# A two-layer token mixer: one more empty step in two side lanes, and small matmuls gathered into fewer steps

## The chip, the cores and the metric

The kernel runs on one core of a Trainium2 chip. The metric is the device time of one launch in microseconds (us). The engines are named as in the profile: PE is TensorE (matmul), PEld its weight loads, DVE is VectorE, ACT is ScalarE, POOL is GpSimd, SP is SyncE, which here issues the weight DMAs.

## The reference, cut to what matters

Two layers over 256 positions and 2048 channels. The even layer mixes with HGRN2 (a gated linear recurrence, 8 heads of 128 keys) and RG-LRU (a gated scan after a causal convolution, 8 blocks of 128) side by side; the odd layer is mLSTM (8 heads, 128 keys, 256 values). Each layer ends with an output projection, a residual add and a gated embedding of a second input `p`.

```python
h = x
for i in range(2):
    hn = rmsnorm(h, norm[i])
    if i == 0:
        q, f, v, z, xb, zb = split(hn @ e_w_in)          # 2048 -> 6 x 1024
        ya = head_rmsnorm(hgrn2(q, f, v, lb)) * silu(z)
        xc = causal_conv(xb, w, b)                        # 4 taps
        r, g = sigmoid(xc @ w_r + b_r), sigmoid(xc @ w_i + b_i)   # per block of 128
        a = exp(-8 * r * softplus(-lam))
        yb = scan(a, sqrt(1 - a * a) * (g * xc)) * silu(zb)
        mix = concat(ya, yb) @ e_w_out
    else:
        q, k, v, og, z, ig, fg = split(hn @ o_w_in)
        q, k = silu(causal_conv(q, k))
        yc = mlstm(q, k, v, ig, log_sigmoid(fg))          # (q k' * weights) v / max(|den|, exp(-m))
        mix = (head_rmsnorm(yc) * sigmoid(og) * silu(z)) @ o_w_out
    h = h + mix
    h = h + sigmoid(h @ ple_gate_w[i]) * rmsnorm(p[i] @ ple_w[i])
return rmsnorm(h)
```

All in fp32.

## The kernel before, in words

**The main line.** Nearly all time goes into projections of 256 tokens by weights that come from memory once. A float32 product is made of three: the weight piece (`raw`, 128x1024, 512 KB, by SP's queue) is rounded by ACT (`whi`, L123), the remainder is taken by DVE (`wlo`, L124), and the activations are kept as `ahl`, a rounded part and a remainder side by side. `whi` and `wlo` have four buffers each, two blocks' worth. `block` (L147) makes 128 output channels for all tokens: 16 matmuls with `whi` (L155, 128x512), then `pump()`, then 16 with `wlo` (L162, 128x256). `merge` (L179, L180) adds the two halves of its bank, `project` (L190) multiplies by the norm's factor. `project_tok` (L193) has tokens on the partitions and two banks: for each of four quarters of the inputs (`kq` 0 to 3) 12 matmuls into the first bank (L208 to L210), `pump()`, and 12 into the second. `gate_tok` calls it for a gate and follows it with a tanh (ACT, L444) and a product (DVE, L445) for each bank.

**The side lanes.** The rest of the work is written as Python generators that stand in named lanes: "att" (HGRN2's attention of four heads, called a pair g here, `attention(g)`), "rg" (`rg_lru(r, xc)`), "mix" (`mix(j)`, mLSTM of two heads), "tr" (`turn`), "fm", "norm" and others. Every `pump()` advances each lane to its next `yield`, and the matmuls of that step stand in PE's program between the `whi` and the `wlo` matmuls of one block. So a `yield` is the unit of delay: it puts what follows it one block later. When a generator of a lane ends, the next one's first step runs in the same pump. The tile scheduler then orders each engine by what is ready, and the casts L123 and L124 have a priority.

**The lanes that the change touches**, by the lines of the kernel before:
- `attention` (L524): `qf = q * f` on DVE (L530, 128x1024), a yield, then five levels B = 1, 2, 4, 8, 16. Each level's matmuls (L546; at B = 1 L541 too) read `qf` and `k`, then DVE multiplies half of `qf` (L553) and half of `k` (L554) by the level's factors and forms the next factors (L556), a yield. After the levels come one more step of matmuls (L605, L610), and `read_out` (from L628) with the values, whose normalisation on DVE is a dozen small operations (L216 to L222, L644, L648) and a product (L650).
- `rg_lru` (L662): waits a step, and then for j = 0, 1 makes two gate products from `xc`, the convolution's output, each of two matmuls in a bank of its own (L674), followed by sigmoids on ACT (L678), and a yield. Then tanh, exp, square (L684 to L690), a square root (L693), and the scan (DVE, L696). `xc` is made by `conv`: one ACT operation (L705) and three of DVE (L708) for each 128 channels.
- `mix` (L864): decay weights, two empty steps, then the scores of two heads (L887, L888; DVE multiplies them by the weights, L889), a yield, then the read-out with the values (L899, L901), from which ACT copies and squares and DVE copies one column (L904), a yield.
- `turn` (L1018): turns two 128x512 halves of the residual by four transposes each (L1023), a yield after each half.

**PSUM.** Three pools: "mm" with three banks for projections, "mx" with three and "st" with two for the side lanes. A side step that takes a bank waits until its last reader is done.

Of the kernel before, what the change touches and what calls it, by code (L numbers as in the profile page):

```python
# [11 lines left out]
F32 = mybir.dt.float32  # L12
# [4 lines left out]
ALU = mybir.AluOpType  # L17
PSUM = bass.MemoryType.PSUM

P = 128  # L20
# [24 lines left out]
def trunk(ctx: ExitStack, tc: tile.TileContext, a, out):  # L45
    nc = tc.nc
    v, s, gp, te, sy = nc.vector, nc.scalar, nc.gpsimd, nc.tensor, nc.sync
# [7 lines left out]
    px = ctx.enter_context(tc.tile_pool(name="px", bufs=3, space=PSUM))  # L55
    pst = ctx.enter_context(tc.tile_pool(name="pst", bufs=2, space=PSUM))
# [7 lines left out]
    def start(lane, gen):  # L64
        lanes.setdefault(lane, []).append(gen)
# [374 lines left out]
    def gate_tok(w, j, act, u):  # L440
# [6 lines left out]
    mx, e0, e1, lb, omb, sp, ez, z2, pol, sp8, spm8 = (small(8, n) for n in (  # L447
        "mx", "e0", "e1", "lb", "omb", "sp", "ez", "z2", "pol", "sp8", "spm8"))
# [37 lines left out]
    with m0_scope:  # L486
# [37 lines left out]
        def attention(g):  # L524
# [2 lines left out]
            Ac = m0.tile([P, 4, P], F32, name="Ac", tag="Ac", bufs=1)  # L527
            C = m0.tile([P, 8, 32], F32, name="C", tag="C", bufs=1)
            qf = m0.tile([P, 1024], F32, name="qf", tag="qf", bufs=1)
            v.tensor_tensor(out=qf, in0=q, in1=f, op=ALU.mult)  # L530
            if g == 0:
                gp.memset(A, 0.0)
# [2 lines left out]
            for B in LEVELS:  # L535
                ps = px.tile([P, 512], F32, name="mx", tag="mx")
                if B == 1:
                    for c in range(8):
                        for x in range(0, P, 32):
                            o = c * P + x  # L540
                            te.matmul(ps[x:x + 32, 128 + c * 32:160 + c * 32], k[:, o:o + 32], q[:, o:o + 32],  # L541
                                      start=True, stop=True)
                for c in range(8):
                    for x in range(0, P, 32):
# [3 lines left out]
                                  start=True, stop=True)  # L548
# [28 lines left out]
            for i in (1, 0):  # L577
                v.tensor_tensor(out=sx[:, :, i], in0=sx[:, :, i + 1], in1=t4[:, :, 0, i + 1], op=ALU.mult)
                j = 3 - i
# [17 lines left out]
            for b in range(2):  # L597
                ps = px.tile([P, 512], F32, name="mx", tag="mx")
# [8 lines left out]
            ps = pst.tile([P, 512], F32, name="st", tag="st")  # L607
# [54 lines left out]
        def rg_lru(r, xc):  # L662
            bw = m0.tile([P, 2, 512], F32, name="bw", tag="bw", bufs=1)
            sy.dma_start(out=bw, in_=a["bw"][r])
            av = m0.tile([P, 1024], F32, name="av", tag="f")
            tt = m0.tile([P, 1024], F32, name="tt", tag="k")
            it = m0.tile([P, 1024], F32, name="it", tag="it", bufs=1)
            yield
            for j in range(2):
                for w, (dst, bias) in enumerate(((av, "bbr"), (it, "bbi"))):  # L670
                    ps = px.tile([P, 512], F32, name="mx", tag="mx")
                    for i in range(2):
                        c = 2 * j + i
                        te.matmul(ps[:, i * T:(i + 1) * T], bw[:, w, c * P:(c + 1) * P], xc[:, c * T:(c + 1) * T],  # L674
                                  start=True, stop=True)
                    for i in range(2):
                        c = 2 * j + i
                        s.activation(dst[:, c * T:(c + 1) * T], ps[:, i * T:(i + 1) * T], AF.Sigmoid,  # L678
                                     bias=pc(bias, 4 * r + c))
                yield  # L680
            for c in range(4):
                b = 4 * r + c
                cc = slice(c * T, (c + 1) * T)
                s.activation(tt[:, cc], av[:, cc], AF.Tanh, scale=sp8[:, b:b + 1])  # L684
                s.activation(av[:, cc], av[:, cc], AF.Exp, scale=spm8[:, b:b + 1])
            v.tensor_tensor(out=it, in0=it, in1=xc, op=ALU.mult)
            for j in range(2):
                sq = tp.tile([P, 512], F32, name="sq", tag="sq")
                jj = slice(j * 512, (j + 1) * 512)
                s.activation(sq, av[:, jj], AF.Square)  # L690
                v.scalar_tensor_tensor(tt[:, jj], sq, 1.0, tt[:, jj], op0=ALU.add, op1=ALU.mult)
            yield
            s.activation(tt, tt, AF.Sqrt, scale=0.25)  # L693
            v.tensor_tensor(out=it, in0=it, in1=tt, op=ALU.mult)
            v.memset(av.rearrange("p (c t) -> p c t", t=T)[:, :, 0:1], 0.0)
            v.tensor_tensor_scan(tt, av, it, 0.0, op0=ALU.mult, op1=ALU.add)  # L696
            res["h", r] = tt
# [13 lines left out]
        vts = [i_proj(0), i_proj(1)]  # L711
# [47 lines left out]
    with tc.tile_pool(name="m1", bufs=2) as m1:  # L759
# [20 lines left out]
        vts = []  # L780
        for j in range(4):
            psv = project_tok(a["ov"], j, acth)

            vt = m1.tile([P, 2, 2, VW], F32, name="vt", tag="vt", bufs=6)
# [9 lines left out]
        ps = pm.tile([P, 512], F32, name="mm", tag="mm")  # L794
        for hf in range(2):
            wt = wp.tile([P, 1024], F32R, name="whi", tag="whi")
# [8 lines left out]
            for kk in range(8):  # L805
                k = hf * 8 + kk
                for i, x in enumerate(acth[k // 2][0:2]):
                    te.matmul(ps[:, 0:T], wt[:, kk * P:(kk + 1) * P], x[:, k % 2],
                              start=(k == i == 0), stop=(k == KT - 1 and i == 1))
# [42 lines left out]
        SC = 0.25 * 128.0 ** -0.5  # L852
# [11 lines left out]
        def mix(j):  # L864

            if j == 0:
                spread(0)
                spread(1)
                yield
            p3 = spr[j]  # L870
            wt = m1.tile([P, 2, 384], F32, name="wt", tag="wt", bufs=1)
            v.tensor_tensor(out=wt[:, :, 0:T], in0=tri2.unsqueeze(1).to_broadcast([P, 2, T]), in1=p3, op=ALU.subtract)
            v.tensor_tensor(out=wt[:, :, T:384], in0=tri2[:, 0:P].unsqueeze(1).to_broadcast([P, 2, P]),
                            in1=p3[:, :, P:T], op=ALU.subtract)
            for i in range(2):
                hd = 2 * j + i
                s.activation(wt[:, i, 0:T], wt[:, i, 0:T], AF.Exp, bias=aT[:, hd:hd + 1])
                s.activation(wt[:, i, T:384], wt[:, i, T:384], AF.Exp, bias=aT[:, 8 + hd:9 + hd])
            if j < 2:
                spread(j + 2)  # L880
            yield
            yield
            scw = m1.tile([P, 2, 384], F32, name="scw", tag="scw", bufs=2)
            for i in range(2):
                q, k = qk[j][:, i * T:(i + 1) * T], qk[4 + j][:, i * T:(i + 1) * T]
                sc = px.tile([P, 512], F32, name="mx", tag="mx")
                te.matmul(sc[:, 0:T], k[:, 0:P], q, start=True, stop=True)  # L887
                te.matmul(sc[:, T:384], k[:, P:T], q[:, P:T], start=True, stop=True)  # L888
                v.scalar_tensor_tensor(scw[:, i, :], sc[:, 0:384], SC, wt[:, i, :], op0=ALU.mult, op1=ALU.mult)  # L889
            yield  # L890

            vt = vts[j]
            nm = m1.tile([P, 2, 512], F32, name="num", tag="vt", bufs=6)
            for i in range(2):
                pool, tag = ((px, "mx"), (pst, "st"))[i]
                for hf in range(2):
                    c = hf * 8 + 2 * j + i
                    ps = pool.tile([P, 512], F32, name="nu", tag=tag)[:, 0:VW]
                    te.matmul(ps, scw[:, i, hf * P:(hf + 1) * P], vt[:, 0, i], start=True, stop=(hf == 0))  # L899
                    if hf:  # L900
                        te.matmul(ps, scw[:, i, T:384], vt[:, 1, i], start=False, stop=True)  # L901
                    o = nm[:, hf, i * 256:(i + 1) * 256]
                    s.copy(o, ps[:, 0:256])
                    v.tensor_copy(den[:, c:c + 1], ps[:, 256:VW])  # L904
                    sq = tp.tile([P, 512], F32, name="sq", tag="sq")[:, 0:256]
                    s.activation(sq, ps[:, 0:256], AF.Square, accum_out=ss[:, c:c + 1])
            nums[j] = nm
            yield

        def mix_norm():  # L910


            t, r, yh = (m1.tile([P, 16], F32, name=n, bufs=1) for n in ("nwt", "nwr", "nwy"))
            s.activation(den, den, AF.Abs)
            v.tensor_tensor(out=den, in0=den, in1=aT[:, 16:32], op=ALU.max)
            v.tensor_scalar(den, den, 1e21, EPS ** 0.5, op0=ALU.min, op1=ALU.mult)
            v.tensor_tensor(out=den, in0=den, in1=den, op=ALU.mult)
            v.scalar_tensor_tensor(den, ss, 1.0 / 256, den, op0=ALU.mult, op1=ALU.add)
            newton(den, t, r, yh)
            for hf in range(2):  # L920
                c = slice(hf * 8, hf * 8 + 8)
                v.tensor_scalar(fac[:, c], r[:, c], norm["rt"][:, hf:hf + 1], 0.25, op0=ALU.mult, op1=ALU.mult)
            yield

        y = {}
        for j in range(4):
            qk[j] = qk_proj(j)
            qk[4 + j] = qk_proj(4 + j)
            start("mix", mix(j))
        start("mix", mix_norm())  # L930
        held = []
        for j in range(4):
# [85 lines left out]
        def turn(q, banks):  # L1018

            for hf in range(2):  # L1020
                ps = px.tile([P, 512], F32, name="mx", tag="mx")
                for i in range(4):
                    te.transpose(ps[:, i * P:(i + 1) * P], hq[q][:, i * T + hf * P:i * T + (hf + 1) * P], ident)  # L1023
                banks.append(ps)
                yield

        def gated(n, ps, tr, pl, hf, on_act=True):
            th = tp.tile([P, 512], F32, name="th", tag="th")[:, 0:pl.shape[1]]
# [182 lines left out]
```

## Time and profile before

| what | us |
| --- | --- |
| median of 3 runs | 1079.74 (1079.16 to 1080.49) |
| the profiled execution | 1078.11 |
| its span | 1076.3 |
| PE busy | 1055.6 |
| DVE busy | 735.1 |
| ACT busy | 584.8 |
| POOL busy | 67.8 |

The profiled execution is one launch; its span goes from the first to the last instruction. A row of a timeline gives the start, the length, the engine and line, the operation with its tiles and shape, the count of equal instructions, and in brackets idle time just before with what ended it. PE writes two records for a matmul of plain float32 operands, so `x8` at L674 is four matmuls. PE's rows overlap (the next matmul starts before the last one's modelled end), so its costs are read from start to start.

### The profile page before, as it was taken

What the parts mean: (1) busy time and instruction counts of PE and PEld (TensorE: products, weight loads), DVE (VectorE), ACT (ScalarE), POOL (GpSimd) and SP (SyncE); (2) the same over time, 40 slices, a digit from 0 to 9 for tenths busy, and PEclk for the clock granted to TensorE, in tenths of its full rate; (3) what the DMA queues carried; (4) which work ended last, traced back from release to release, by engine and by line L of the source; (5) the groups of instructions that cost most, each with busy time, mean ns of one, the idle gap of its engine ahead of it and who ended that gap; (6) DMA issues with size and microseconds to landing.
All of it is one profiled execution on the core that took longest, in us unless ns stands there. A gap on an engine that the chain in (4) does not pass through costs nothing.

```text
span 1076.3 us, 16798 instructions
## 1 busy us (share of the span) xinstructions
PE 1055.6 (98%) x6500; PEld 910.4 (85%) x6500; DVE 735.1 (68%) x1106; ACT 584.8 (54%) x863; POOL 67.8 (6%) x72
## 2 busy tenths in 40 slices
PE   7999999999999999999999999999999999999996
PEld 6888888887888888888888888888888888888886
DVE  6868978877767557777544887855456677555665
ACT  7565455688654435556444666654445554434543
POOL 0140400000000000112000000000000000000111
PEclk9999999999999999999999999999999999999998
DMA  9667444445655555555654655545555755555552
GB/s 337 166 230 217 153 160 149 154 138 194 240 195 193 193 186 188 185 189 194 195 193 158 216 188 167 176 157 195 195 195 190 247 184 181 196 192 176 181 176 79
DMA packets 56576, 201.76 MB, mean 187 GB/s; under 512 B 6472, under 2 KB 6864, under 8 KB 56496
## 3 DMA queue, kind: packets, MB, share of 16 engines
q1 hardware_dynamic: 54720, 195.04, 54.1%
q0 software_dynamic: 1776, 5.65, 1.8%
q8 instruction: 51, 0.84, 0.3%
q14 instruction: 29, 0.24, 0.1%
HBM read 198.55 MB, written 2.11 MB: 186 GB/s over the span
## 4 chain that ended last, share of the span: by engine, by line
PE 93%; DVE 2%; ACT 2%; issue 1%; DMA 1%; SPq 0%; DVEq 0%; ACTq 0%
PE mm L155 31%; PE mm L162 16%; PE mm L208 12%; PE mm L209 12%; PE mm L210 12%; DVE wlo L124 1%; PE mm L1065 1%; PE mm L1064 1%; PE mm L1063 1%; PE nu L899 1%; PE mx L546 1%; DMA raw<-in_pw_dram 1%; PE mx L428 0%; ACT whi L123 0%; PE mm L143 0%
## 5 line engine op out<-in xcount | busy, mean ns | idle before, releaser
L124 DVE TENSOR_TENSOR wlo<-raw,whi 128x1024 fp32r<-128x1024 f32 (+1 forms) x361 | 444.9, 1255 | 257.9 <-ACT whi L123 145.7
L123 ACT CAST whi<-raw 128x1024 fp32r<-128x1024 f32 (+1 forms) x361 | 377.5, 1048 | 333.9 <-PE mm L155 163.4
L155 PE MATMUL mm<-ahl,whi 128*128 128x512 f32 x1536 | 367.8, 391 | 0.0
L155 PEld LDWEIGHTS mm<-ahl,whi 128*128 128x128 f32 x1536 | 282.0, 188 | 55.7 <-DVE ahl L139 0.6
L208 PE MATMUL mm<-whi,ahl 128*128 128x512 f32 x608 | 238.7, 393 | 0.0
L210 PE MATMUL mm<-whi,ahl 128*128 128x512 f32 x608 | 236.7, 389 | 0.0
L209 PE MATMUL mm<-wlo,ahl 128*128 128x512 f32 x608 | 236.7, 389 | 0.0
L162 PE MATMUL mm<-ahl,wlo 128*128 128x256 f32 x1536 | 201.8, 284 | 0.0
L162 PEld LDWEIGHTS mm<-ahl,wlo 128*128 128x128 f32 x1536 | 195.7, 191 | 6.2
L210 PEld LDWEIGHTS mm<-whi,ahl 128*128 128x128 f32 x608 | 114.1, 188 | 24.0
L208 PEld LDWEIGHTS mm<-whi,ahl 128*128 128x128 f32 x608 | 114.2, 188 | 23.3
L209 PEld LDWEIGHTS mm<-wlo,ahl 128*128 128x128 f32 x608 | 114.2, 188 | 23.0
L179 ACT COPY sm<-mm 128x256 f32<-128x256 f32 x64 | 23.7, 371 | 43.8 <-PE mm L162 43.8
L180 DVE TENSOR_TENSOR mg<-mm,sm 128x256 f32<-128x256 f32 x64 | 26.6, 416 | 0.8 <-ACT sm L179 0.7
L772 DVE SCALAR_TENSOR_TENSOR qk<-mg,prm,qk 128x255 f32<-128x255 f32 (+2 forms) x48 | 21.5, 480 | 5.7 <-ACT qk L769 5.5
L261 POOL TENSOR_TENSOR acc<-acc,sq 128x512 f32<-128x512 f32 x6 | 9.7, 1621 | 193.8 <-ACT sq L260 193.8
L1051 POOL TENSOR_TENSOR pl<-pl,row 128x512 f32<-128x512 f32 x6 | 9.2, 1527 | 191.3 <-ACT sq L1035 191.3
L1063 PE MATMUL mm<-whi,ahl 128*128 128x256 f32 x64 | 18.3, 285 | 0.0
L1065 PE MATMUL mm<-whi,ahl 128*128 128x256 f32 x64 | 18.1, 283 | 0.0
L1064 PE MATMUL mm<-wlo,ahl 128*128 128x256 f32 x64 | 18.1, 283 | 0.0
L190 DVE TENSOR_TENSOR mg<-mg,hrs 128x512 f32<-128x512 f32 (+1 forms) x25 | 17.8, 714 | 0.3
L143 PE MATMUL mm<-ahl,whi 128*128 128x256 f32 x32 | 10.0, 314 | 7.4 <-ACT whi L123 7.4
(293 smaller groups left out, 772.1 us busy)
## 6 DMA issues: line engine op xcount, KB each, us to landing
raw<-in_ew_dram SPq DMA_DIRECT2D x64, 512.0 KB, 5.0
raw<-in_g_dram SPq DMA_DIRECT2D x56, 512.0 KB, 4.1
raw<-in_eo_dram SPq DMA_DIRECT2D x32, 512.0 KB, 4.7
raw<-in_ov_dram SPq DMA_DIRECT2D x32, 512.0 KB, 4.8
raw<-in_oqk_dram SPq DMA_DIRECT2D x32, 512.0 KB, 4.6
raw<-in_oog_dram SPq DMA_DIRECT2D x32, 512.0 KB, 4.5
raw<-in_oz_dram SPq DMA_DIRECT2D x32, 512.0 KB, 4.3
raw<-in_oo_dram SPq DMA_DIRECT2D x32, 512.0 KB, 4.1
```

The source lines that it names most:

```text
L123: last["act"] = s.copy(h, r).ins
L124: last["dve"] = v.tensor_tensor(out=l, in0=r, in1=h.bitcast(F32), op=ALU.subtract).ins
L155: last["pe"] = te.matmul(ps, parts[k // 8][0][:, c:c + P], act[k // 2][2][:, (k % 2) * 512:(k % 2 + 1) * 512], start=(k == 0), stop=False).ins
L162: last["pe"] = te.matmul(ps[:, T:2 * T], parts[k // 8][1][:, c:c + P], act[k // 2][0][:, k % 2], start=False, stop=(k == KT - 1)).ins
L179: s.copy(small, ps[:, T:2 * T])
L180: v.tensor_tensor(out=dst, in0=ps[:, 0:T], in1=small, op=ALU.add)
L208: te.matmul(ps[hf], xh, wh, start=(k == 0), stop=False)
L209: te.matmul(ps[hf], xh, wl, start=False, stop=False)
L210: last["pe"] = te.matmul(ps[hf], xl, wh, start=False, stop=(k == KT - 1)).ins
L1063: te.matmul(ps[hf], xh, wh, start=(k == 0), stop=False)
L1064: te.matmul(ps[hf], xh, wl, start=False, stop=False)
L1065: last["pe"] = te.matmul(ps[hf], xl, wh, start=False, stop=(k == KT - 1)).ins
```

## The change

Four edits; lines of the changed kernel are up to 13 higher.

```diff
@@ attention @@
             qf = m0.tile([P, 1024], F32, name="qf", tag="qf", bufs=1)
+            yield
             v.tensor_tensor(out=qf, in0=q, in1=f, op=ALU.mult)
@@ rg_lru @@
             yield
+            yield
             for j in range(2):
                 for w, (dst, bias) in enumerate(((av, "bbr"), (it, "bbi"))):
-                    ps = px.tile([P, 512], F32, name="mx", tag="mx")
+                    pool, tag = (pst, "st") if j == w == 1 else (px, "mx")
+                    ps = pool.tile([P, 512], F32, name="rg", tag=tag)
...
-                yield
+            yield
@@ mix @@
-            scw = m1.tile([P, 2, 384], F32, name="scw", tag="scw", bufs=2)
+            sc_ = m1.tile([P, 2, 384], F32, name="scw", tag="scw", bufs=2)
...
+            scws[j] = sc_
+            if j:
+                mix_out(j - 1)
+            yield
+
+        scws = {}
+
+        def mix_out(j):
+            vt, scw = vts[j], scws[j]
             nm = m1.tile([P, 2, 512], F32, name="num", tag="vt", bufs=6)
             for i in range(2):
-                pool, tag = ((px, "mx"), (pst, "st"))[i]
                 for hf in range(2):
+                    pool, tag = ((px, "mx"), (pst, "st"))[i != hf]
...
+        def mix_last():
+            mix_out(3)
             yield
...
             start("mix", mix(j))
+        start("mix", mix_last())
         start("mix", mix_norm())
@@ turn @@
                 banks.append(ps)
-                yield
+            yield
```

In `attention` the whole generator is one step later for each pair. In `rg_lru` both j's gate products are in the second of the two places, four banks at once, the last of them from the "st" pool. In `mix` the scores of heads 2j and 2j + 1 share a step with the read-out of the two heads before, and the read-out's four banks come from "mx", "st", "st", "mx" instead of "mx", "mx", "st", "st"; the last read-out has a step of its own. In `turn` both halves are turned in one step.

On PE, at the start of the first pair's attention (L541, L546: level 1, then level 2; L155 and L162 are the projection's blocks), before:

```order
L162 MATMUL mm<-ahl,wlo 128x256 x16
L155 MATMUL mm<-ahl,whi 128x512 x16
L541 MATMUL mx<-q,k 32x32 x32
L546 MATMUL mx<-qf,k 32x16 x32
L162 MATMUL mm<-ahl,wlo 128x256 x16
L155 MATMUL mm<-ahl,whi 128x512 x16
L546 MATMUL mx<-qf,k 32x16 x32
L162 MATMUL mm<-ahl,wlo 128x256 x16
```

and in the changed kernel, from the same block on (L542, L547):

```order
L162 MATMUL mm<-ahl,wlo 128x256 x16
L155 MATMUL mm<-ahl,whi 128x512 x16
L162 MATMUL mm<-ahl,wlo 128x256 x16
L155 MATMUL mm<-ahl,whi 128x512 x16
L542 MATMUL mx<-q,k 32x32 x32
L547 MATMUL mx<-qf,k 32x16 x32
L162 MATMUL mm<-ahl,wlo 128x256 x16
L155 MATMUL mm<-ahl,whi 128x512 x16
L547 MATMUL mx<-qf,k 32x16 x32
```

The level steps come one block later.

On DVE, at the same place (L517 makes `q`, L530 `qf`, L553 and L554 the first rewriting of `qf` and `k`), before:

```order
L190 TENSOR_TENSOR mg<-mg,hrs 128x512
L517 SCALAR_TENSOR_TENSOR q<-mg,omb,th 128x256 x2
L530 TENSOR_TENSOR qf<-q,f 128x1024
L124 TENSOR_TENSOR wlo<-raw,whi 128x1024 x2
L180 TENSOR_TENSOR mg<-mm,sm 128x256
L556 TENSOR_TENSOR tot_1425<-tot_1332 128x256
L553 TENSOR_TENSOR qf<-qf,f 128x512
L554 TENSOR_TENSOR k<-k,f 128x512
```

and now (L531, L554, L555):

```order
L517 SCALAR_TENSOR_TENSOR q<-mg,omb,th 128x256 x2
L531 TENSOR_TENSOR qf<-q,f 128x1024
L124 TENSOR_TENSOR wlo<-raw,whi 128x1024 x2
L180 TENSOR_TENSOR mg<-mm,sm 128x256
L557 TENSOR_TENSOR tot_1386<-f 128x512
L124 TENSOR_TENSOR wlo<-raw,whi 128x1024 x2
L180 TENSOR_TENSOR mg<-mm,sm 128x256
L557 TENSOR_TENSOR tot_1473<-tot_1386 128x256
L190 TENSOR_TENSOR mg<-mg,hrs 128x512
L507 TENSOR_SCALAR f<-f,omb,lb 128x256 x2
L554 TENSOR_TENSOR qf<-qf,f 128x512
L555 TENSOR_TENSOR k<-k,f 128x512
```

`qf` stays right behind `q`, the first factors (L556, now L557) and the rewriting have moved behind it, and in front of the rewriting stand a L190 and two L507 that were behind it.

On DVE, at the convolution for the second half of RG-LRU (L708, six instructions; L696 is the first half's scan, L648 and L650 belong to the second pair's read-out), before:

```order
L694 TENSOR_TENSOR it<-it,tt 128x1024
L124 TENSOR_TENSOR wlo<-raw,whi 128x1024 x2
L648 TENSOR_SCALAR hnr<-hnr,rth 128x4 x2
L708 SCALAR_TENSOR_TENSOR xc<-mg,prm,xc 128x255
L650 TENSOR_TENSOR o<-o,hnr 128x1024
L708 SCALAR_TENSOR_TENSOR xc<-mg,prm,xc 128x254
L708 SCALAR_TENSOR_TENSOR xc<-mg,prm,xc 128x255
L708 SCALAR_TENSOR_TENSOR xc<-mg,prm,xc 128x253
L708 SCALAR_TENSOR_TENSOR xc<-mg,prm,xc 128x254
L696 SCALAR_TENSOR_TENSOR tt<-av,it 128x1024
L124 TENSOR_TENSOR wlo<-raw,whi 128x1024 x2
L708 SCALAR_TENSOR_TENSOR xc<-mg,prm,xc 128x253
```

and now (L711):

```order
L190 TENSOR_TENSOR mg<-mg,hrs 128x512
L694 SCALAR_TENSOR_TENSOR tt<-sq,tt 128x512
L698 MEMSET av 128x4
L711 SCALAR_TENSOR_TENSOR xc<-mg,prm,xc 128x255
L711 SCALAR_TENSOR_TENSOR xc<-mg,prm,xc 128x254
L711 SCALAR_TENSOR_TENSOR xc<-mg,prm,xc 128x255
L711 SCALAR_TENSOR_TENSOR xc<-mg,prm,xc 128x253
L711 SCALAR_TENSOR_TENSOR xc<-mg,prm,xc 128x254
L711 SCALAR_TENSOR_TENSOR xc<-mg,prm,xc 128x253
L124 TENSOR_TENSOR wlo<-raw,whi 128x1024 x2
L645 TENSOR_SCALAR hss<-hss 128x8
L216 TENSOR_SCALAR hnt<-hss 128x8
L218 TENSOR_SCALAR hny<-hss 128x8
```

The six convolution instructions stand together, ahead of the read-out's normalisation (L645, L216, L218) and of the scan, which follows later as L699.

More of the change, by code (lines that the diff above doesn't have):

```diff
@@ L888, in mix @@
                 te.matmul(sc[:, T:384], k[:, P:T], q[:, P:T], start=True, stop=True)
-                v.scalar_tensor_tensor(scw[:, i, :], sc[:, 0:384], SC, wt[:, i, :], op0=ALU.mult, op1=ALU.mult)
+                v.scalar_tensor_tensor(sc_[:, i, :], sc[:, 0:384], SC, wt[:, i, :], op0=ALU.mult, op1=ALU.mult)
+            scws[j] = sc_
+            if j:
+                mix_out(j - 1)
             yield
-            vt = vts[j]
+        scws = {}
+        def mix_out(j):
+            vt, scw = vts[j], scws[j]
             nm = m1.tile([P, 2, 512], F32, name="num", tag="vt", bufs=6)
             for i in range(2):
-                pool, tag = ((px, "mx"), (pst, "st"))[i]
                 for hf in range(2):
+                    pool, tag = ((px, "mx"), (pst, "st"))[i != hf]
                     c = hf * 8 + 2 * j + i
```

## The prediction

> **What bounds the kernel now.** I read the page first: the span, the busy shares of the engines, and the shares of the chain that ended last.
>
> ```profile
> span 1076.3 us, 16798 instructions
> PE 1055.6 (98%) x6500; PEld 910.4 (85%) x6500; DVE 735.1 (68%) x1106; ACT 584.8 (54%) x863; POOL 67.8 (6%) x72
> PE 93%; DVE 2%; ACT 2%; issue 1%; DMA 1%; SPq 0%; DVEq 0%; ACTq 0%
> ```
>
> TensorE (PE) is busy for 98% of the span and is 93% of the last chain. The change adds and removes no matmul, so it can only move time that TensorE spends waiting, or lets pass between two matmuls. The waits of TensorE, summed by what it waited for, say how much there is:
>
> ```profile
> PE mm L143 <- ACT whi L123: 7.4, 2, 6.1
> PE mx L674 <- DVE xc L708: 2.3, 1, 2.3
> PE mx L546 <- DVE qf L530: 1.9, 1, 1.9
> ```
>
> The first row (7.4 us in two waits) is the start-up, which no edit touches. The other two, one wait each, sit in lanes that the change edits: the gate products of RG-LRU (L674), and the first level of attention (L546). Elsewhere TensorE never waits, so a step that is only made shorter or split has nothing to win but a few hundredths of a us, while a step that comes too early for its operands costs its whole lateness.
>
> **The extra step in attention.** The timeline of TensorE at the first pair's first level, and two steps on:
>
> ```profile
> 119.14 0.84 PE L541 MATMUL mx<-q,k 128*32 128x32 f32 x64
> 121.86 0.73 PE L546 MATMUL mx<-qf,k 128*32 128x16 f32 x64 [1.88 <-DVE qf L530]
> 122.53 2.17 PE L162 MATMUL mm<-ahl,wlo 128*128 128x256 f32 x16
> 124.54 3.81 PE L155 MATMUL mm<-ahl,whi 128*128 128x512 f32 x16
> 128.28 0.74 PE L546 MATMUL mx<-qf,k 128*32 128x16 f32 x64
> ```
>
> The step takes 122.53 - 119.14 = 3.39 us. The same step of the second pair, without a wait, takes 177.31 - 176.09 = 1.22:
>
> ```profile
> 176.09 0.73 PE L541 MATMUL mx<-q,k 128*32 128x32 f32 x62
> ...
> 177.31 2.18 PE L162 MATMUL mm<-ahl,wlo 128*128 128x256 f32 x16
> ```
>
> So the wait costs 3.39 - 1.22 = 2.17 us. VectorE (DVE) shows why it is there:
>
> ```profile
> 117.41 2.18 DVE L517 SCALAR_TENSOR_TENSOR q<-mg,omb,th 128x256 f32<-128x256 f32 x2 [0.70 <-ACT th L514]
> 119.63 2.18 DVE L530 TENSOR_TENSOR qf<-q,f 128x1024 f32<-128x1024 f32 x1
> 121.73 2.35 DVE L124 TENSOR_TENSOR wlo<-raw,whi 128x1024 fp32r<-128x1024 f32 x2
> ```
>
> `qf` ends at 119.63 + 2.18 = 121.81, and the matmul starts at 121.86. With the extra yield the product stays where it is in VectorE's order (right behind L517) and its readers come one block later. A block without a side step runs from 122.53 to 128.28, that is 5.75 us, so the readers come at about 119.14 + 5.75 = 124.9, some 3 us after `qf`. The wait goes whole: -2.17. The second pair waited for nothing and gains nothing.
>
> What is late next is the rest of the level steps, whose operands `qf` and `k` are rewritten between two steps (L553, L554), because other work now stands ahead of them in VectorE's queue: L190 and two L507 at the first pair, convolutions (L708) or a pair of L124 at the second. The prices, and the smallest margin that the profile of before has:
>
> ```profile
> L190 DVE TENSOR_TENSOR mg<-mg,hrs 128x512 f32<-128x512 f32 x23 | 17.0, 739 | 0.3
> L507 DVE TENSOR_SCALAR f<-f,omb,lb 128x256 f32<-128x256 f32 x8 | 3.1, 422 | 1.3 <-ACT f L503 1.3
> 125.27 0.68 DVE L554 TENSOR_TENSOR k<-k,f 128x512 f32<-128x512 f32 x1
> 188.17 0.68 DVE L554 TENSOR_TENSOR k<-k,tot 128x512 f32<-128x512 f32 x1
> 189.50 0.74 PE L546 MATMUL mx<-qf,k 128*32 128x16 f32 x64
> 188.77 0.47 DVE L708 SCALAR_TENSOR_TENSOR xc<-mg,prm,xc 128x254 f32<-128x254 f32 x1
> ```
>
> At the first pair's second level `k` is ready at 125.95 and needed at 128.28, a margin of 2.33 us; there L190 (0.74) and two L507 (0.84) ahead of it leave 0.75. At the second pair `k` is ready at 188.85 and needed at 189.50, a margin of 0.65; one more convolution (0.47) ahead of it leaves 0.18. No step of the eight is forced to wait, but two or three are within what my sums miss. I take 0.25 us for all of them, between 0 and 1.6 (one step whose `k` falls behind the pair of L124 quoted above: 2.35 - 0.75).
>
> **The gate products in one step.** For the second half of RG-LRU, TensorE now does:
>
> ```profile
> 233.21 1.89 PE L674 MATMUL mx<-xc,bw 128*128 128x256 f32 x8
> 234.74 0.58 PE L208 MATMUL mm<-whi,ahl 128*128 128x512 f32 x1
> ...
> 240.40 1.02 PE L674 MATMUL mx<-xc,bw 128*128 128x256 f32 x4
> 243.73 1.13 PE L674 MATMUL mx<-xc,bw 128*128 128x256 f32 x4 [2.31 <-DVE xc L708]
> 244.51 0.58 PE L208 MATMUL mm<-whi,ahl 128*128 128x512 f32 x1
> ```
>
> Eight records take 234.74 - 233.21 = 1.53 us in the step without a wait and 244.51 - 240.40 = 4.11 in the one with it. The wait costs 2.58 us. VectorE is late for it by its own order:
>
> ```profile
> 237.17 1.66 DVE L708 SCALAR_TENSOR_TENSOR xc<-mg,prm,xc 128x254 f32<-128x254 f32 x4
> 238.75 2.28 DVE L696 TENSOR_TENSOR_SCAN tt<-av,it 128x1024 f32<-128x1024 f32 x1
> 240.95 2.33 DVE L124 TENSOR_TENSOR wlo<-raw,whi 128x1024 fp32r<-128x1024 f32 x2
> 243.20 0.47 DVE L708 SCALAR_TENSOR_TENSOR xc<-mg,prm,xc 128x253 f32<-128x253 f32 x1
> ```
>
> The last of six convolution instructions stands behind the scan (2.28) and a pair of L124 (2.33). In the new order all six come together, ahead of the scan and of the normalisation of the second pair's attention read-out, and the products all come at the later of the two places, a quarter of a projection later. So `xc` is there first, with 2.28 + 2.33 = 4.6 us of other work no longer ahead of it: -2.58.
>
> What is new in this step: four banks at once. Four groups need three banks of one pool and one of the other, and at the first half the third group waits until ScalarE (ACT) has read the first (two sigmoids, 0.84 us), while TensorE has some 1.15 us of other gate products (three quarters of 1.53). I take 0.1, between 0 and 0.84. Behind it, the order of `gate_tok` for the second pair changes: 18 matmuls before it needs its second bank where it was 21, that is 3 x 0.23 = 0.7 us sooner (16 of that size run from 124.54 to 128.28). That bank is free when ScalarE's tanh and VectorE's product with it are done, which the fewer matmuls may not cover:
>
> ```profile
> 215.94 1.28 ACT L678 ACT_TABLE_LOAD   x1
> 217.23 0.84 ACT L678 ACTIVATE av<-mx,prm 128x256 f32<-128x256 f32 x2
> 256.72 1.28 DVE L445 SCALAR_TENSOR_TENSOR u<-u,mm 128x512 f32<-128x512 f32 x2
> ```
>
> The first of two L445 ends at about 257.4 and all of it stays as late relative to TensorE, but for one table load less in front (1.28). I take a wait of 0.3, between 0 and 0.7.
>
> The table load takes 1.28 us and the next activation starts 0.01 behind its end. [...]
>
> **Scores with read-out, and the transposes.** In mLSTM no step waits before, so moving work into one step saves only what an excursion from the projection costs. Four gate records alone took 244.51 - 243.73 = 0.78, eight together 1.53: 2 x 0.78 - 1.53 = 0.03 us for each step merged. Nine are merged (two of RG-LRU, three of mLSTM, four of transposes): at most -0.27, I take -0.2. Their cover is VectorE: the fourth bank of a merged step is one that the step's own first scores fill, and L889 must have read it.
>
> ```profile
> 661.03 0.59 PE L887 MATMUL mx<-qk 128*128 128x256 f32 x2
> ...
> 662.25 2.16 PE L162 MATMUL mm<-ahl,wlo 128*128 128x256 f32 x16
> 667.91 1.03 PE L899 MATMUL nu<-vt,scw 128*128 128x257 f32 x4
> ...
> 669.21 1.03 PE L899 MATMUL nu<-vt,scw 128*128 128x257 f32 x4
> 661.98 1.11 DVE L889 SCALAR_TENSOR_TENSOR scw<-mx,wt 128x384 f32<-128x384 f32 x2
> ```
>
> Scores take 662.25 - 661.03 = 1.22 us; the fourth bank is wanted 1.30 + 0.43 us later, 2.95 after the first score. L889's first half is done 661.98 + 0.55 - 661.03 = 1.5 after it. Its margin of 1.45 is less than two L124, more than one: 0.1 for three steps, between 0 and 1.5. The two transposes of a tile go into two different banks, freed several us before: 0. No DMA moves past another in SP's or POOL's queue, and each lane has as many products as before.
>
> **The sum**, in the profiled execution: -2.17 - 2.58 - 0.2 + 0.25 + 0.1 + 0.3 + 0.1 = -4.2 us. That execution took 1078.11 us (span 1076.3), so 1073.9; it was 1.6 under the median of the runs, 1079.74, from which the forecast is taken: 1079.74 - 4.2 = **1075.5 us**.
>
> **Rivals.** How busy VectorE is around the second pair's first level steps:
>
> ```profile
> 175.00:186.00 11.00, 11.00 (x248) 9.51 (x247) 10.35 (x24) 4.97 (x7) 0.00 (x0) 1.00 0.54 192
> ```
>
> (Behind the length of 11.00 us: the busy time of TensorE, of its weight loads, of VectorE, ScalarE and GpSimd, then the clock and the DMA.)
>
> A measurement of this kernel can tell about 0.2%, 2.2 us, from no change; the bounds of "same" are 1077.6 and 1081.9.
>
> *One wait goes, the other moves.* The late `qf` only shifts: VectorE does the same work in the stretch, and the second level waits 2.17 us in place of the first. For it: VectorE runs from 117.41 to 124.08 in the rows above without a pause. Against it: the block between gives it 5.75 us, and L190 and two L507 are only 1.6. Gain 2.58 + 0.2 - 0.75 = 2.0: 1077.7.
>
> *Level steps become bound by VectorE, and the kernel slower.* In both pairs the rewriting of `k` falls behind a pair of L124 that stood behind it: 2.35 us against a margin of 0.75, 1.6 late at each of eight steps, 12.8 us in all: 1079.74 - 4.95 + 12.8 = 1087.6. VectorE's 10.35 of 11.00 us around the second pair speaks for it. Against it: one such place already has the pair ahead of `k` (the row at 188.17) and kept 0.65. It is slower than before from (4.95 + 2.2) / 8 = 0.9 us late at each step.
>
> *The change does nothing to the waits*, since both are set by VectorE's total work: 1079.7. Against it speaks the order of VectorE, in which the waited-for instructions no longer stand behind the scan.
>
> **Chances.** Forecast 0.76; one wait goes and one moves, 0.12 (half of it within 0.2%); no gain, 0.08; slower, 0.04. So faster 0.76 + 0.06 = 0.82, same 0.06 + 0.08 = 0.14, slower 0.04. The range: low end all new waits zero and the last 0.07 of the merges, 1079.74 - 5.0 = 1074.7, less the 0.6 by which the runs of before lay under their median: 1074.1. High end: the new waits at their larger bounds in part (+2.5 in place of 0.75), 1077.4, and half a us of the first rival: 1078.0.
>
> **What would show it.** Right: no row of TensorE waiting for `qf` or `xc`; 1.22 us for the first level step; the sixteen gate records of a half in one piece, about 3.1 us; waits of well under 0.5 us at level steps or at the second bank of `gate_tok`. Wrong: new rows of TensorE waiting for `k`, for the sigmoids or for L889 (now L892) that add to more than 2 us, or a wait of 2 us at the second level.

## The result, and the profile after

The changed kernel takes 1073.99 us (median of 6 runs, 1073.45 to 1075.74) against 1079.55 for the one before (6 runs, 1077.04 to 1080.88): a ratio of 0.995, 95% interval 0.9939 to 0.9961, that is 4.2 to 6.6 us less. The forecast was 1075.5 in a range of 1074.1 to 1078.0; 1073.99 is just beneath its low end and the gain, 5.6, is larger than the 4.2 forecast. Its profiled execution took 1074.36 us.

The page of the changed kernel, span and busy time, and the waits of TensorE (by line and what it waited for: us in all, times, the longest):

```profile
span 1072.6 us, 16798 instructions
PE 1056.2 (98%) x6500; PEld 911.4 (85%) x6500; DVE 733.7 (68%) x1106; ACT 583.4 (54%) x861; POOL 68.1 (6%) x72
PE mm L143 <- ACT whi L123: 6.6, 2, 6.0
PE mm L208 <- DVE u L445: 0.7, 1, 0.7
```

Both waits of before are gone, and TensorE is as busy as it was. One new wait stands in their place, 0.7 us at L208 for VectorE's product L445: the second bank of the second gate, as foreseen, but larger. The first level step of attention on TensorE, and VectorE at the same place:

```profile
124.92 0.73 PE L542 MATMUL mx<-q,k 128*32 128x32 f32 x62
...
126.14 2.18 PE L162 MATMUL mm<-ahl,wlo 128*128 128x256 f32 x16
115.45 2.17 DVE L517 SCALAR_TENSOR_TENSOR q<-mg,omb,th 128x256 f32<-128x256 f32 x2 [0.70 <-ACT th L514]
117.66 2.20 DVE L531 TENSOR_TENSOR qf<-q,f 128x1024 f32<-128x1024 f32 x1
```

The step takes 126.14 - 124.92 = 1.22 us, as the second pair's did, and `qf` is there at 119.86, 5 us early. The gate products of RG-LRU's second half, and the convolution and the scan on VectorE:

```profile
236.74 3.61 PE L677 MATMUL rg<-xc,bw 128*128 128x256 f32 x16
240.00 0.58 PE L208 MATMUL mm<-whi,ahl 128*128 128x512 f32 x1
227.36 2.70 DVE L711 SCALAR_TENSOR_TENSOR xc<-mg,prm,xc 128x255 f32<-128x255 f32 x6
238.35 2.28 DVE L699 TENSOR_TENSOR_SCAN tt<-av,it 128x1024 f32<-128x1024 f32 x1
```

Sixteen records take 3.26 us where before they took 1.53 and 4.11. All six convolution instructions are done at 230.06, before the scan starts.

Matmul by matmul (the start of each of the 5216 projection matmuls, after against before) the profiled execution is 0.22 us later at the end of the start-up, gains 2.18 at the first level step, 2.58 at the gate products, gives 0.97 back at the gate's second bank, loses 0.06 in the three merged mLSTM steps and gains 0.30 in the four of transposes. That is 4.0 us outside the start-up, 3.75 in all, and 1.8 less than the medians differ. The experiments had to find out which edit did what, and where the rest is.

### The profile page after: what moved, and what is told of

Read it like the earlier page. It is cut to its first block, busy times and chain, and to the rows that moved or that the text cites. A ratio compares the mean times of both kernels' runs of the same rounds, so it can differ in the third digit from the quotient of the medians.

```text
span 1072.6 us, 16798 instructions
## 1 busy us (share of the span) xinstructions
PE 1056.2 (98%) x6500; PEld 911.4 (85%) x6500; DVE 733.7 (68%) x1106; ACT 583.4 (54%) x861; POOL 68.1 (6%) x72
## 4 chain that ended last, share of the span: by engine, by line
PE 94%; ACT 3%; DVE 1%; DMA 0%; issue 0%; SPq 0%; DVEq 0%; ACTq 0%
PE mm L155 32%; PE mm L162 17%; PE mm L208 12%; PE mm L209 12%; PE mm L210 12%; ACT whi L123 1%; PE mm L1078 1%; PE mm L1077 1%; PE mm L1076 1%; PE nu L908 1%; PE mx L547 1%; PE mx L428 0%; DMA raw<-in_pw_dram 0%; PE mm L143 0%; PE mm L145 0%; PE mm L144 0%
## 5 line engine op out<-in xcount | busy, mean ns | idle before, releaser
L124 DVE TENSOR_TENSOR wlo<-raw,whi 128x1024 fp32r<-128x1024 f32 (+1 forms) x361 | 444.8, 1255 | 243.4 <-ACT whi L123 135.4
L155 PE MATMUL mm<-ahl,whi 128*128 128x512 f32 x1536 | 367.8, 391 | 0.0
L155 PEld LDWEIGHTS mm<-ahl,whi 128*128 128x128 f32 x1536 | 282.0, 188 | 55.7 <-DVE ahl L139 0.6
L208 PE MATMUL mm<-whi,ahl 128*128 128x512 f32 x608 | 238.2, 392 | 0.7 <-DVE u L445 0.7
L162 PE MATMUL mm<-ahl,wlo 128*128 128x256 f32 x1536 | 201.5, 284 | 0.0
L162 PEld LDWEIGHTS mm<-ahl,wlo 128*128 128x128 f32 x1536 | 195.9, 191 | 6.4
L208 PEld LDWEIGHTS mm<-whi,ahl 128*128 128x128 f32 x608 | 114.2, 188 | 24.3 <-DVE u L445 1.1
L180 DVE TENSOR_TENSOR mg<-mm,sm 128x256 f32<-128x256 f32 x64 | 26.7, 417 | 0.0
L190 DVE TENSOR_TENSOR mg<-mg,hrs 128x512 f32<-128x512 f32 (+1 forms) x25 | 17.3, 692 | 0.4
L139 DVE TENSOR_TENSOR ahl<-hq,ahl 128x512 fp32r<-128x512 f32 x16 | 10.7, 689 | 9.5 <-ACT ahl L138 9.5
```

Source lines behind the costliest of these rows:

```text
L124: last["dve"] = v.tensor_tensor(out=l, in0=r, in1=h.bitcast(F32), op=ALU.subtract).ins
L155: last["pe"] = te.matmul(ps, parts[k // 8][0][:, c:c + P], act[k // 2][2][:, (k % 2) * 512:(k % 2 + 1) * 512], start=(k == 0), stop=False).ins
L162: last["pe"] = te.matmul(ps[:, T:2 * T], parts[k // 8][1][:, c:c + P], act[k // 2][0][:, k % 2], start=False, stop=(k == KT - 1)).ins
L180: v.tensor_tensor(out=dst, in0=ps[:, 0:T], in1=small, op=ALU.add)
L208: te.matmul(ps[hf], xh, wh, start=(k == 0), stop=False)
```

## The experiments

Nine kernels, and the one before once more. The one before was run again beside them, in three groups; its medians there were 1079.24 (21 runs, experiments 1, 2, 7 and 8), 1078.99 (23; 3 to 6) and 1079.06 (17; 9 and 10).

**1. The attention step alone.**

```diff
             qf = m0.tile([P, 1024], F32, name="qf", tag="qf", bufs=1)
+            yield
             v.tensor_tensor(out=qf, in0=q, in1=f, op=ALU.mult)
```

> The kernel before with the extra yield in attention alone. Theory of the prediction (each edit removes its own wait): the wait for qf goes (2.17 us), the wait for xc stays at about 2.3, so 2.2 us faster than before. Rival: the later step also takes the second pair's read-out, its normalisation and product, from ahead of the convolution on VectorE, since in the order of this kernel the six convolution instructions stand together ahead of the scan: both waits go, 4.75 us faster. On the new wait of 0.7 us for the second bank of the gate: if it comes from the gathered gate products, it is absent here; if it comes from the later read-out, it is here too.

Measured: 1073.97 us, ratio 0.9947 (0.9933 to 0.996), the whole gain. Waits of TensorE, in all:

```profile
PE mm L143 <- ACT whi L123: 6.3, 2, 6.1
```

Only the start-up is left. VectorE shows why the second wait went with the first:

```profile
225.59 2.45 DVE L709 SCALAR_TENSOR_TENSOR xc<-mg,prm,xc 128x255 f32<-128x255 f32 x6
227.95 1.22 DVE L124 TENSOR_TENSOR wlo<-raw,whi 128x1024 fp32r<-128x1024 f32 x1
229.09 2.29 DVE L697 TENSOR_TENSOR_SCAN tt<-av,it 128x1024 f32<-128x1024 f32 x1
231.28 1.21 DVE L124 TENSOR_TENSOR wlo<-raw,whi 128x1024 fp32r<-128x1024 f32 x1
232.40 0.17 DVE L645 TENSOR_SCALAR hss<-hss 128x8 f32<-128x8 f32 x1
```

The read-out's normalisation (from L645) now comes behind the convolution, because the read-out itself is a block later; the six instructions run in one piece and end at 228.04. The theory that each edit removes its own wait has fallen. Nor is there a wait at the gate's second bank: the gathered gate products bring it, though not by themselves, since experiment 2 has them and no such wait.

**2. The gathered gate products alone.**

```diff
             yield
+            yield
             for j in range(2):
...
-                    ps = px.tile([P, 512], F32, name="mx", tag="mx")
+                    pool, tag = (pst, "st") if j == w == 1 else (px, "mx")
+                    ps = pool.tile([P, 512], F32, name="rg", tag=tag)
...
-                yield
+            yield
```

> The kernel before with the gathered gate products of RG-LRU and their empty step alone. Theory of the prediction: the wait for xc goes and the one for qf stays, 2.6 us faster. Rival: the convolution still stands behind the read-out, a pair of casts and the scan on VectorE, so TensorE still waits for xc by 1.5 to 3 us at the one place where all gate products now are, and the wait for qf stays too: within 1 us of before.

Measured: 1078.17, ratio 0.9985 (0.9976 to 0.9994), 1.1 us less in the medians, of which the trace shows 0.24 past the start-up. Its waits, and the end of the convolution on VectorE:

```profile
PE mx L546 <- DVE qf L530: 1.6, 1, 1.6
PE rg L676 <- DVE xc L710: 1.4, 1, 1.4
PE rg L676 <- ACT A L614: 0.5, 1, 0.5
...
237.09 2.35 DVE L124 TENSOR_TENSOR wlo<-raw,whi 128x1024 fp32r<-128x1024 f32 x2
239.36 0.87 DVE L710 SCALAR_TENSOR_TENSOR xc<-mg,prm,xc 128x253 f32<-128x253 f32 x2
240.15 2.28 DVE L698 TENSOR_TENSOR_SCAN tt<-av,it 128x1024 f32<-128x1024 f32 x1
242.35 0.98 DVE L710 SCALAR_TENSOR_TENSOR xc<-mg,prm,xc 128x254 f32<-128x254 f32 x2
```

`xc` still comes behind the scan, and a new wait for a bank (0.5 us, until ScalarE has copied it, L614) eats part of what is won. The rival holds, at its edge.

**3. The later read-out alone**, to part it from the shift of the level steps:

```diff
             s.copy(Ac.rearrange("p c t -> p (c t)"), ps)
             yield
+            if g:
+                yield
             read_out(g, A, Ac, vts[g])
```

> The kernel before with one empty step ahead of the second pair's read-out and no other edit: no step of the attention levels moves and qf comes as late as before. Theory now: TensorE waited for xc because the read-out's normalisation and product stood among the convolution's instructions on VectorE; with the read-out one step later the six stand together, and this wait alone goes: 2.6 us faster by the trace from start to start, the wait for qf (1.4 to 1.9 us in three profiles of kernels with that step) stays. Rival: the shift of the whole attention did it, by moving the level updates out of the way; then the wait for xc stays at 2.3 us and the kernel is as before.

Measured: 1075.4, ratio 0.9964 (0.9952 to 0.9976). Of the waits past the start-up one is left:

```profile
PE mx L546 <- DVE qf L530: 1.9, 1, 1.9
```

The wait for `xc` is gone with this one empty step, and the trace gains 2.45 us there. So it is the read-out, not the shift of the levels. The median gains 3.6, a us more than the trace, as in the whole change.

**4. Without GpSimd's products**, for the other wait. This kernel leaves out the norm factor of the even layer's embedding.

```diff
         for j, pl in enumerate(pls):
-            x3 = pl.rearrange("p (j t) -> p j t", j=2)
-            gp.tensor_tensor(out=x3, in0=x3, in1=rs.unsqueeze(1).to_broadcast([P, 2, T]), op=ALU.mult)
             if j % 2:
                 yield
```

> The kernel before without GpSimd's eight products of the embedding's norm (L332; the embedding of the even layer lacks that factor). Theory: qf is late because VectorE's operations next to those products take up to twice their usual time (1.77 for 0.74 us, 2.18 for two of L517 at 1.29 apiece in place of 0.44, 2.18 for 1.22); without them qf is ready some 3 us sooner and the wait for it goes with no extra step, 2.2 us faster. Rival: qf is late because q is, by VectorE's order and ScalarE's sigmoid; then the wait stays.

Measured: 1076.32, ratio 0.9979 (0.997 to 0.9988), 2.7 us less in the medians. Its waits past the start-up, and VectorE where `qf` is made:

```profile
PE mx L672 <- DVE xc L706: 2.3, 1, 2.3
...
113.67 0.69 DVE L190 TENSOR_TENSOR mg<-mg,hrs 128x512 f32<-128x512 f32 x1
115.06 0.88 DVE L515 SCALAR_TENSOR_TENSOR q<-mg,omb,th 128x256 f32<-128x256 f32 x2 [0.70 <-ACT th L512]
115.97 1.23 DVE L528 TENSOR_TENSOR qf<-q,f 128x1024 f32<-128x1024 f32 x1
```

The wait for `qf` is gone without any extra step: 0.88 us for the two of L515 (L517 before) and 1.23 for the product L528 (L530), where they took 2.18 each. It was GpSimd's eight products beside them that made `qf` late. In the profile of the changed kernel, L180, which reads one operand from PSUM, takes its usual 0.41 us in the same stretch in which L190 takes 1.34:

```profile
112.97 0.41 DVE L180 TENSOR_TENSOR mg<-mm,sm 128x256 f32<-128x256 f32 x1
113.41 1.34 DVE L190 TENSOR_TENSOR mg<-mg,hrs 128x512 f32<-128x512 f32 x1
```

In the first profile of before, the operations that slowed beside the products have all their operands in SBUF and took 1.8 to 2.6 times as long: L190 1.77 us for 0.69, two of L517 2.18 for 0.88, L530 2.18 for 1.23. Whether it is the place of the operands that matters, no run shows.

**5. Slower level steps**, for the rival that the steps come too early.

```diff
                 v.tensor_tensor(out=kv, in0=kv, in1=tv[:, :, 1:2].to_broadcast([P, n, B]), op=ALU.mult)
+                for _ in range(2):
+                    v.tensor_tensor(out=kv, in0=kv, in1=kv, op=ALU.max)
```

> The changed kernel with two more operations of VectorE behind each rewriting of k (each the maximum of k's half with itself, 0.61 us from start to start, values unchanged). Theory: the margins in the trace of the changed kernel are 2.13, 3.94, 1.35 and 4.3 us at the first pair's level steps and 0.14, 3.64, 0.58 and 4.1 at the second's; 1.22 us more shows as waits of 1.1 and 0.6 at the two tight steps and up to 0.9 at the steps behind the levels: 1.7 to 2.6 us slower than the changed kernel. Rival (the slower rival of the prediction): VectorE bounds these stretches, and each of ten steps is 1.2 us later: 12 us slower.

Measured: 1081.02, ratio 1.0017 to before (1.0008 to 1.0026), 7 us slower than the changed kernel. Neither theory had it right. TensorE's waits past the start-up, VectorE ahead of the worst, and TensorE's granted clock around it (the third from last column of the windows, behind the busy times):

```profile
PE mx L547 <- DVE k L557: 3.4, 2, 3.0
PE mm L208 <- DVE u L445: 1.3, 1, 1.3
...
131.15 0.69 DVE L555 TENSOR_TENSOR k<-k,f 128x512 f32<-128x512 f32 x1
131.76 2.35 DVE L124 TENSOR_TENSOR wlo<-raw,whi 128x1024 fp32r<-128x1024 f32 x2
134.03 0.68 DVE L557 TENSOR_TENSOR k<-k 128x512 f32<-128x512 f32 x1
...
136.00:140.00 4.00, 4.00 (x73) 3.96 (x64) 2.89 (x5) 0.00 (x0) 0.00 (x0) 0.50 0.39 134
```

Two of the steps wait, not ten, so VectorE doesn't bound these stretches. But at the first pair's second level, which had a margin of 2.13 us, the scheduler put a pair of L124 between the rewriting and the added operations: 3.0 us late instead of in time. That is the mechanism of the slower rival, at one step. And behind this wait TensorE ran at half its clock for some 6 us, which cost 2.6 us more.

**6. The kernel before once more.**

```diff
(no edit)
```

> The kernel before once more, for a second profile. The two profiled executions before and after stand 3.75 us apart, the medians 5.6. Theory: the first profile of before was a good one at the start-up (7.4 us of waits for the first cast) or at its two later waits, and this one is longer there, by 1 to 2 us, with the steady parts equal. Rival: the same to 0.3 us, and the difference of the medians has another place.

Measured: one run, 1080.22 us. Its wait for `xc` is as long as in the first profile (2.3 us) and the one for `qf` shorter (1.3), but it is 1.6 us longer past the wait for `xc`:

```profile
244.15 1.30 PE L674 MATMUL mx<-xc,bw 128*128 128x256 f32 x4 [2.31 <-DVE xc L708]
244.93 0.95 PE L208 MATMUL mm<-whi,ahl 128*128 128x512 f32 x1
245.68 0.63 PE L209 MATMUL mm<-wlo,ahl 128*128 128x512 f32 x1
246.10 0.63 PE L210 MATMUL mm<-whi,ahl 128*128 128x512 f32 x1
...
248.54 0.40 PE L210 MATMUL mm<-whi,ahl 128*128 128x512 f32 x1
248.78 0.39 PE L208 MATMUL mm<-whi,ahl 128*128 128x512 f32 x1
...
244.00:248.00 4.00, 3.85 (x11) 3.10 (x12) 0.09 (x1) 2.68 (x4) 0.00 (x0) 0.62 0.62 226
```

From 245.68 the matmuls start every 0.42 us in place of 0.23, until 248.5; the granted clock in that window is 0.62. In the first profile of before it is 1.00 in the same four us:

```profile
244.00:248.00 4.00, 4.00 (x19) 3.33 (x19) 0.63 (x1) 3.96 (x6) 0.00 (x0) 1.00 0.55 197
```

So the wait for `xc` costs 2.58 us, or 4.2. Of the four profiles with this wait at 2.3 us two show the half clock (this one and experiment 7) and two don't (the first of before, and experiment 4 with a mean of 1.00 from 110 to 260 us). Waits of 1.9 us or less never showed it in nine profiles, the one of 3.0 us did.

How often it happens can be read from the mean granted clock of each execution over its whole span. That mean also holds a half clock at the end, behind TensorE's last matmul (the last 7.1 us in the first profile of before, the last 5.2 in that of the changed kernel), so 0.997 can be either: the first profile of before has it without the half clock behind the wait, this one with it; 0.996 and less was seen only in kernels with a wait of 2.3 us or more:

| kernels | executions | of these at 0.995 or 0.996 |
| --- | --- | --- |
| before (longest wait past the start-up 2.3 us) | 61 | 39 |
| experiment 7 (2.3 us; without the execution of 3552 us) | 10 | 7 |
| experiment 4 (2.3 us) | 10 | 4 |
| the changed one and experiments 1, 2, 3, 8, 9, 10 (1.9 us or less) | 49 | 0 |
| experiment 5 (3.0 us) | 10 | 10 |

Of the 61 executions of before, the 39 at 0.995 or 0.996 have a median of 1079.32 us and the 14 at 0.998 one of 1077.89. The rival, another place for the difference, has a part as well: the start-up was 1.1 us longer (and the wait for `qf` 0.6 shorter).

**7. The merged mLSTM steps and transposes alone** (the last two edits of the change).

```diff
-                yield
+            yield
```

(`turn`; `mix` as in the change)

> The kernel before with the merged steps of mLSTM and of the transposes alone. Theory: 0.03 us for each of seven merged steps, at most 0.2 us faster, both waits as before; in the trace of the whole change the three merged mLSTM steps cost 0.06 us more and the four of transposes 0.07 less each. Rival: more than that, 1.5 us or so, since the medians of before and after stand 5.6 us apart and the two profiled executions 3.75.

Measured: 1079.3 (11 executions, one of them of 3552 us that the ratio leaves out), ratio 0.9996 (0.9986 to 1.0006): no difference to be told. The merged mLSTM steps cost 0.06 us in the trace and the merged transposes save 0.2 to 0.3, as in the whole change. Its profile shows the half clock behind the wait for `xc`: a mean of 0.58 from 244 to 248 us.

**8. The gate's tanh first.** The changed kernel with

```diff
+        with tc.high_priority(offset=400):
-        for hf in range(2):
+            for hf in range(2):
...
```

around the tanh and the product of `gate_tok`.

> The changed kernel with the gate's tanh and product at the priority of the casts. Theory: the wait of 0.7 us (0.97 by start to start) for the second bank of the second gate is there because the tanh stands behind the exponentials and squares of RG-LRU on ScalarE; with the priority it is gone and the kernel 0.9 us faster than the changed one, 1073.1 against 1074.0. Rival: the wait is set by VectorE, whose product stands behind a pair of casts, or the casts that now stand behind the tanh are late instead: no gain.

Measured: 1072.72, ratio to before 0.9939 (0.9926 to 0.9953), 1.3 us under the changed kernel's median. The only wait left is that of the start-up:

```profile
PE mm L143 <- ACT whi L123: 6.2, 2, 5.9
```

The new wait of the change was the tanh's place on ScalarE, as the theory had it. The medians' intervals overlap, so that this version is the faster one is shown by the trace (0.97 us) and not by the medians.

**9. Attention step and transposes, without the gathered products.**

> The kernel before with the extra step in attention and the merged transposes, without the gathered gate products and without the merged mLSTM steps. Theory now: the step in attention removes both waits (4.75 us), the transposes save 0.07 us in each of four places, and the wait at the gate's second bank (0.97 us), which came with the gathered gate products, is not there: 4.6 us outside the start-up by the trace of the step alone, 4.9 here, so 0.9 more than the whole change in the trace, 1073.1 in the median against 1074.0. Rival: the gathering has a use that the parts alone don't show, and this is slower than the whole change.

The edits are those of 1 and of `turn` in 7. Measured: 1074.15, ratio 0.9957 (0.9942 to 0.9971), within what the whole change and the step alone show, and not the 0.9 us better that was expected. The trace has no wait at the gate's bank, but one that experiment 1, with the same attention, did not have:

```profile
PE mx L547 <- DVE k L555: 0.4, 1, 0.4
```

It is the first pair's fourth level. In this execution GpSimd's products ran from 107.98 to 121.8 us, in experiment 1 from 105.53 to 118.4, and `k` is ready at 145.3 for a step due at 145.1, where experiment 1 has 143.0 for 143.6. A margin of half a us here depends on the execution; in the profile of experiment 10 the products start later still, at 109.72, and the same wait is 0.8 us.

**10. The gate products gathered, without the empty step.** The changed kernel with

```diff
             yield
-            yield
             for j in range(2):
```

> The changed kernel without the empty step of RG-LRU, its gate products still gathered, so all of them stand at the first of the two places. Theory: the step is what the gathering needs, since xc's last instructions end at about 230 to 233 us in VectorE's order and the products come some 5.2 us (23 matmuls) sooner than at 236.5: a wait of 1 to 1.5 us for xc at the second half, none at the first, and no wait at the gate's second bank, since the sigmoids come 5 us sooner: about as fast as the changed kernel. Rival: with the read-out out of the way xc is early enough even there, and the kernel is 0.9 us faster than the changed one.

Measured: 1075.33, ratio 0.9968 (0.9959 to 0.9977), 1.3 us slower than the changed kernel, whose interval just touches this one. Its waits past the start-up:

```profile
PE rg L676 <- DVE xc L710: 0.9, 1, 0.9
PE mx L547 <- DVE k L555: 0.8, 1, 0.8
```

As the theory had it, the gathered products need the step (0.9 us for `xc`, somewhat less than the 1 to 1.5 expected), and the gate's bank is no longer waited for. It was expected to be about as fast as the changed kernel; the second wait, for `k`, which is the one of experiment 9, was not foreseen.

## Why the prediction was right, and where it was not

- *The two waits go, 2.17 and 2.58 us, and nothing of like size comes.* Right in place and size: 2.18 and 2.58 by start to start.
- *The gathered products remove the wait for `xc`.* Wrong, though the sum did not show it. The step of the prediction saw the right thing in the order, that the convolution no longer stands behind the scan, and put it to the edit of RG-LRU. Alone, that edit leaves it behind the scan (experiment 2); the later read-out alone takes it out (experiment 3). The extra step in attention has the whole gain (experiment 1).
- *New waits of 0.75 us.* The gate's bank was mis-sized: 0.7 as a row and 0.97 from start to start, against 0.3 and a bound of 0.7. The bound counted the three matmuls fewer and took the tanh to be as late as before; experiment 8 shows that its place on ScalarE was what made the wait. The four banks at once, 0.1 in the sum, cost nothing: the sixteen gate records start 0.22 us apart throughout. A table load took 1.28 us here too, and the next activation starts 0.02 us behind its end.

```profile
245.33 1.28 ACT L688 ACT_TABLE_LOAD   x1
246.63 0.51 ACT L688 ACTIVATE av<-av,spm 128x256 f32<-128x256 f32 x1
251.86 0.67 ACT L444 ACTIVATE u<-mm,rth 128x512 f32<-128x512 f32 x1
253.31 0.50 PE L208 MATMUL mm<-whi,ahl 128*128 128x512 f32 x1 [0.69 <-DVE u L445]
```

- *Level steps 0.25, between 0 and 1.6.* 0 in the profile of the changed kernel, 0.4 and 0.8 in two others with the same attention. The margin at the first pair's second level was 2.13 us, not 0.75: L190 and the two L507 in front of it were done early.
- *Merged steps: -0.2, and 0.1 for the mLSTM bank.* -0.30 from the transposes, +0.06 from mLSTM, 0 from RG-LRU.
- *The profiled execution stands for the median.* This step failed, and it is why the gain was larger than forecast. The sum priced the wait for `xc` by one execution in which the clock stayed up. In another of the same kernel (experiment 6) it also cost 1.6 us of half clock. By the mean clocks of experiment 6 that is at least 39 of 61 executions and at most the 47 that are not at 0.998, so 1.0 to 1.2 us on average (an estimate: 1.6 x 39/61 and 1.6 x 47/61): 4.0 + 1.0 to 1.2 = 5.0 to 5.2 us, within the measured 4.2 to 6.6. The remaining half a us, a part of which is the start-up of each execution, is left open.

Taken from the profiled execution itself, the sum gave 1073.9, and the changed kernel measured 1073.99: neither profile has the half clock behind a wait. Some of that closeness is luck, because the new waits were 1.03 us in place of 0.75 and stood almost all in one place, and the merged steps won 0.1 more than was taken.

The rival "one wait goes, the other moves" and the one without effect are out by the profile of the changed kernel; the slower one needs two more operations of VectorE in each level (experiment 5) to show at one step.

## What to carry to other kernels

Where the bound engine waits twice, look for what stands ahead of both late operands in the other engine's order before giving each edit its own gain: an empty step for one lane also moves its later steps out of another lane's way. A long wait of TensorE (2.3 us here) can cost more than its row says, since the matmuls behind it may run at half clock (in two of four profiles here, for 1.6 us more in the one that was priced); a single profile does not show how often they do, but the mean clock of many executions does. A margin of half a us on VectorE is none when GpSimd's work beside it starts at another time in each execution (from 105.5 to 109.7 us in seven profiles here).

## What the runs showed of the hardware that was not expected

- At TensorE's waits of 2.3 us (two of four profiles) and 3.0 us (one of one) the granted clock fell to half, for 3.4 us in the first two and 6.8 in the third, of which 0.7 still in the wait (worked out from the mean clocks of windows of four us): 0.42 us from start to start of 128x512 matmuls in place of 0.23 in the first two. Waits of 0.4 to 1.9 us left it at 1.00 (the mean from 110 to 260 us, in the five profiles that have no longer one there). Why it falls in some executions with the same wait and not in others, no run shows.
- The start-up has a slow pace too, and the windows' clock does not show it: in the first profile the matmuls of L143 to L145 (128x256) start every 0.21 us until 11.1 us and every 0.12 from there, with 1.00 for both stretches; sixteen of L162, of the same shape, take 3.58 us at the half clock of experiment 5, 0.22 apiece. The trace's own record of the clock begins where the pace changes, at 11.1 us, and in the profile of the changed kernel, where the pace changes at 12.7, it begins there. In their first 40 us the twelve profiles have from 174 matmuls (experiment 10) to 187 (experiment 1), so by an estimate from these counts the start-up alone makes executions differ by up to 3 us (13 matmuls at 0.23).
- VectorE's operations with all operands in SBUF took up to 2.6 times their time beside GpSimd's products (L190: 1.77 for 0.69 us; two of L517: 2.18 for 0.88), and L180, with an operand from PSUM, 0.41 as elsewhere (0.42 in the mean of its 64).
